# A two-layer DeltaNet and attention block on one core: shared decay buffers, decay exponents on ACT, the late modulation as one DVE product

## Chip, cores and metric

One core of one Trainium2 chip. The metric is the device time of one execution in microseconds (us), and the median of several runs is compared. The profile is of one execution. Its engines are PE (TensorE, matmul; PEld is its weight load), DVE (VectorE), ACT (ScalarE), POOL (GpSimd) and SP (SyncE, which here only issues DMAs). ACT issues DMAs too, from its own instruction queue.

## What is computed

Two layers over 256 context and 256 latent tokens, D = 2048. Layer 0 mixes with a bidirectional gated DeltaNet (16 key heads, 32 value heads, width 128), layer 1 with differential attention. What matters here is this:

```
mod   = silu(c) @ ada_w[i] + ada_b[i]          # (D) @ (D, 3D): shift, scale, gate; once for c, once for c_ctx
h     = rmsnorm(x) * (1 + scale) + shift       # per layer, latent and context tokens
g     = -exp(a_log) * softplus(...)            # log decay, per token and head
gc    = cumsum(g) within a chunk
decay = exp(gc[i] - gc[j]) where i >= j, else 0
lower = beta * (k k^T) * decay, strictly lower # inverted as (I + lower)^-1
a     = (q k^T) * decay
x     = x + gate * mixer(h)
```

## The kernel before, in words

All is kept transposed: features on the 128 partitions, the 512 tokens (context, then latent) on the free axis. Every large product is three fp32r matmuls: a weight tile is split into a high part (ACT, a cast at L185) and a low part (POOL, or for every other piece after the loop DVE, L187).

**Start** (L284 to L330). The 16 tiles of x are loaded on SP (L298), squared on ACT and summed on DVE to the norm. The shift and scale of layer 0 are computed on TensorE by `ada_pair` (L173) from 64 loads of 512 KB (`ada_load`, L164, on SP); sixteen pairs, two of them before every two tiles of h. Three projections run along while h is made (L313).

**Gates** (`gates`, L361). From a small projection come beta and the cumulated log decay: `gct` (the cumulated decay minus lnb, L449) and `lnb` (L443), both with tokens on partitions, and the decay rows in DRAM (`gc_d`, L435).

**The DeltaNet loop** (L486 to L997). Four streams are interleaved by `Drive`, a small event simulation written into the kernel: it emits the matmul groups in the order of their modelled readiness and rank. `stream_m` (L728) makes the masked matrices m for each head pair g and half and inverts 16x16 blocks on DVE (`block_inv`, L703); `stream_lev` (L760) widens the inverse on TensorE over PSUM tiles iv (R on DVE at L786, T and U on ACT at L803 and L804); `stream_at` (L807) makes q k^T times decay; `stream_b` (L832) runs the chunk recurrence over PSUM tiles sb and so (y and yb, x0, x, S: L879 to L926). `filler` (L652) runs the input projections in what is left of TensorE. Both `stream_m` and `stream_at` call `decay` (L682) for each of 4 chunks and 16 head pairs, 128 times in all. It loads the decay rows of four (direction, head) pairs by two broadcast DMAs on SP (L686), subtracts and clamps in four DVE instructions with per-partition operands (L692), and takes the exponential on ACT (L694). The tile has one buffer per caller (tags grm and gra); `scaled` (L697) is its last reader, on DVE.

**The late modulation.** The gate of layer 0 and all of layer 1's modulation, 64 column tiles of 128, are not needed early. `ada_pieces` (L150) cuts each column tile into eight pieces of 256 inputs. A piece is loaded on ACT's queue into one of two buffers (tag ra, L135), along with the two condition rows, broadcast, for every four column tiles (L158); for each of the two conditions POOL multiplies (L138) and ACT sums with an accumulating copy (L139). That is 64 x 8 = 512 loads and 1024 products. 24 column tiles are emitted among the loop's streams with the lowest rank but one (L995), 24 between the output projection's tiles (L1041, L1067), 16 between the heads of layer 1 (L1146).

**After the loop.** The output projection in two halves (L1032, L1053), the norm and h of layer 1 (L1078), layer 1 with eight heads (L1131 to L1207), its output projection and the final norm.

**What orders the work.** The program is written in the Tile layer. It allocates buffers by tag (as many at a time as `bufs` says), places the waits, and orders each engine's instructions ahead of time: a list scheduler with a timeline simulation (L1287) takes the ready instruction that stands first in the program. So work of low rank or of a later stage can be placed early on an engine that is idle in that simulation. On the chip every queue then runs strictly in that order.

Of the kernel before, what the change touches and what calls it, by code (L numbers as in the profile page):

```python
# [10 lines left out]
F32 = mybir.dt.float32  # L11
F32R = mybir.dt.float32r
F16 = mybir.dt.float16
BF16 = mybir.dt.bfloat16
AF = mybir.ActivationFunctionType
# [5 lines left out]
P = 128  # L21
T = 512
NCH = 4
# [38 lines left out]
def body(ctx, tc, D, d, out):  # L62
# [70 lines left out]
    def ada_part(l, ct, q, cr, acc, NK):  # L133
        r = wp.tile([P, NK], F32, tag="ra", name=f"aw{l}_{ct}_{q}", bufs=2)
        nc.scalar.dma_start(r, d["adaw"][l, ct, :, q * NK:(q + 1) * NK])  # L135
        for s in range(2):
            pr = wp.tile([P, NK], F32, tag="rp", name=f"rp{l}_{ct}_{q}{s}", bufs=1)
            nc.gpsimd.tensor_tensor(pr, r, cr[:, s], ALU.mult)  # L138
            nc.scalar.activation(pr, pr, AF.Copy, accum_out=acc[:, s, q:q + 1])  # L139

# [9 lines left out]
    def ada_pieces(lcs):  # L150
        NK = 256
        NQ = D // NK
        accs = {lc: cst.tile([P, 2, NQ], F32, name=f"al{lc[0]}_{lc[1]}", tag="al", bufs=5) for lc in lcs}
        for q in range(NQ):
            yield
            cr = wp.tile([P, 2, NK], F32, name=f"cr{lcs[0]}{q}", tag="cr", bufs=2)
            for s in range(2):
                nc.scalar.dma_start(cr[:, s], sc_d[s:s + 1, q * NK:(q + 1) * NK].to_broadcast([P, NK]))  # L158
            for lc in lcs:
                ada_part(*lc, q, cr, accs[lc], NK)  # L160
        for lc in lcs:
            ada_fin(*lc, accs[lc])
# [98 lines left out]
    gp = gp_cm.__enter__()  # L261
    gct, eg, kd, egl, lnb = (gp.tile([P, NCH, 2, HV], F32, name=n) for n in ("gct", "eg", "kd", "egl", "lnb"))
    zt = gp.tile([P, P], F16, name="zt")
# [32 lines left out]
    with tc.high_priority():  # L296
        for kt in range(KT):
            nc.sync.dma_start(xt[kt], d["xT"][:, kt])  # L298
        nc.scalar.activation(acc0, xt[0], AF.Square)
# [6 lines left out]
        for k0 in range(0, KT, SK):  # L306
            for kind in range(2):
                pr = kind * HKT + k0 // 2
                ada_pair(0, pr, ada_load(0, pr, ta, "ar", 8), (gq, tr)[np_ % 2](), ta)
                np_ += 1  # L310
# [50 lines left out]
    def gates(ps):  # L361
# [65 lines left out]
        for a in range(2):  # L427
            p3 = (gq, tr)[a]()
            for c in range(2):
# [12 lines left out]
        nc.vector.tensor_scalar(t2[0], bt, -1.0, None, ALU.mult)  # L442
        nc.vector.tensor_scalar(lnb, softplus(0), -1.0, None, ALU.mult)  # L443
        tc.keep_in_program_order(nc.scalar.activation(eg, p1v, AF.Exp))
# [3 lines left out]
        nc.vector.tensor_copy(raw, p1v)  # L448
        nc.vector.tensor_tensor(gct, raw, lnb, ALU.subtract)  # L449
        e = tl("be", sh)  # L450
# [231 lines left out]
    def decay(g, c, s, tag):  # L682
        gr = dl.tile([P, 4, P], F32, tag=tag, name=f"{tag}{g}{c}", bufs=1)
        gsrc = gc_d[c].rearrange("(d h) i -> d h i", d=2)
# [4 lines left out]
        for u in range(4):  # L689
            dd, h = divmod(u, 2)  # L690
            j = 2 * g + h
            nc.vector.tensor_scalar(gr[:, u], gr[:, u], gct[:, c, dd, j:j + 1], lnb[:, c, dd, j:j + 1],  # L692
                                    ALU.subtract, ALU.min)
        nc.scalar.activation(gr, gr, AF.Exp)  # L694
        return gr
# [7 lines left out]
    def block_inv(g, half, m16):  # L703
# [7 lines left out]
        pr = dl.tile([64, 16, 16], F32, tag="bP", name=f"bP{nm}", bufs=1)  # L711
        TU = dl.tile([64, 2, 16, 16], F16, tag="bT", name=f"bT{nm}", bufs=1)
        nc.vector.tensor_scalar(X[:32], bk[:32].rearrange("p j i -> p i j"), -1.0, None, ALU.mult)
# [587 lines left out]
```

## Time and profile before

| | us |
|---|---|
| median of 3 runs (3129.51 to 3135.29) | 3134.51 |
| the profiled execution | 3130.73 |
| its span, first to last instruction | 3128.9 |
| PE busy in the span | 2817.8 |
| POOL, DVE, ACT busy | 2012.8, 1955.8, 1872.4 |
| mean granted clock of TensorE | 0.963 |

The span is what the engines show; about 2 us of the execution lie around it. Busy times are unions over an engine's instructions, and DMA-issuing instructions are not counted as busy. A wait row says how long an engine sat idle before instructions of one group, and what ended that. The wait is put down to what came last. A granted clock of 1.00 is 2.4 GHz, 0.50 would be 1.2 GHz.

### The profile page before, as it was taken

What the parts mean: (1) busy time and instruction counts of PE and PEld (TensorE: products, weight loads), DVE (VectorE), ACT (ScalarE), POOL (GpSimd) and SP (SyncE); (2) the same over time, 40 slices, a digit from 0 to 9 for tenths busy, and PEclk for the clock granted to TensorE, in tenths of its full rate; (3) what the DMA queues carried; (4) which work ended last, traced back from release to release, by engine and by line L of the source; (5) the groups of instructions that cost most, each with busy time, mean ns of one, the idle gap of its engine ahead of it and who ended that gap; (6) DMA issues with size and microseconds to landing.
All of it is one profiled execution on the core that took longest, in us unless ns stands there. A gap on an engine that the chain in (4) does not pass through costs nothing. (4 is left out here: it accounts for less than half of the span.)

```text
span 3128.9 us, 52162 instructions
## 1 busy us (share of the span) xinstructions
PE 2817.8 (90%) x16178; PEld 2239.7 (72%) x16178; DVE 1955.8 (63%) x4287; ACT 1872.4 (60%) x5466; POOL 2012.8 (64%) x2370
## 2 busy tenths in 40 slices
PE   5788988988988988988898888899998999999998
PEld 2465767766766766766776666688687888888897
DVE  2178688688678677688578678632335654544454
ACT  4345766766766666766666666654556666654353
POOL 2366777777767777777777777466565666752334
PEclk8899999999999999999999999999999999999999
DMA  9646555456545545445456445667744555543345
GB/s 339 235 100 139 124 127 130 127 119 135 126 118 133 134 116 139 117 125 139 117 126 137 121 120 138 173 178 207 238 147 120 162 155 162 160 142 109 115 130 164
DMA packets 510312, 457.03 MB, mean 146 GB/s; under 512 B 241744, under 2 KB 380752, under 8 KB 510032
## 3 DMA queue, kind: packets, MB, share of 16 engines
q1 hardware_dynamic: 299456, 342.48, 37.7%
q10 hardware_dynamic: 210576, 111.22, 14.9%
q8 instruction: 127, 2.08, 0.3%
q14 instruction: 153, 1.25, 0.1%
HBM read 427.18 MB, written 26.36 MB: 145 GB/s over the span
## 5 line engine op out<-in xcount | busy, mean ns | idle before, releaser
L139 ACT ACTIVATE rp<-rp 128x256 f32<-128x256 f32 x1024 | 426.8, 417 | 298.2 <-POOL rp L138 292.6
L717 DVE TENSOR_TENSOR bP<-bX,bY 64x1 f32<-64x1 f32 (+14 forms) x480 | 225.1, 469 | 22.0 <-ACT bY L715 14.2
L139 ACT ACTIVATION_READ_ACCUMULATOR rp<-rp 128x1 f32 x1024 | 194.2, 190 | 0.0
L692 DVE TENSOR_SCALAR grm<-grm,gct,lnb 128x128 f32<-128x128 f32 x256 | 133.2, 563 | 84.8 <-DMA grm<-gc_d 84.1
L692 DVE TENSOR_SCALAR gra<-gra,gct,lnb 128x128 f32<-128x128 f32 x256 | 116.0, 493 | 85.0 <-DMA gra<-gc_d 84.7
L786 DVE TENSOR_TENSOR R<-iv,lv 128x512 f16<-128x512 f32 x192 | 127.1, 680 | 28.7 <-PE iv L83 28.5
L83 PEld LDWEIGHTS <-m 128*128 128x128 f16 x1024 | 76.2, 100 | 78.7 <-issue 71.5
L694 ACT ACTIVATE grm<-grm 128x512 f32<-128x512 f32 x64 | 40.3, 630 | 129.1 <-DVE grm L692 125.3
L719 DVE TENSOR_REDUCE bY<-bP 64x1 f32<-64x1 f32 (+14 forms) x480 | 108.6, 226 | 8.0
L750 POOL TENSOR_TENSOR ma<-ma,cs 128x512 f32<-128x512 f32 x64 | 86.5, 1352 | 32.3 <-DVE ma L700 30.0
L83 PE MATMUL iv<-T,m 128*128 128x128 f16 x768 | 74.3, 225 | 32.5 <-DMA T<-tu_d 19.1
L83 PE MATMUL iv<-U,R 128*128 128x128 f16 x768 | 76.9, 227 | 28.5 <-DVE R L786 26.4
L694 ACT ACTIVATE gra<-gra 128x512 f32<-128x512 f32 x64 | 40.4, 631 | 103.8 <-DVE gra L692 103.7
L83 PEld LDWEIGHTS <-R 128*128 128x128 f16 x768 | 48.8, 101 | 70.9 <-DVE R L786 37.9
L224 DVE TENSOR_TENSOR hlo<-mh,hhi 128x512 fp32r<-128x512 f32 x32 | 25.9, 833 | 114.9 <-ACT hhi L223 87.8
L83 PE MATMUL sb<-yb,uf 128*128 128x128 bf16 x512 | 55.5, 225 | 32.5 <-DVE yb L910 20.9
L803 ACT CAST T<-iv 128x512 f16<-128x512 f32 x128 | 74.1, 579 | 16.2 <-PE iv L83 12.5
L753 POOL TENSOR_TENSOR ml<-ma,m 128x512 bf16<-128x512 f32 x64 | 75.3, 1177 | 6.2 <-ACT m L752 5.3
L83 PEld LDWEIGHTS <-uf 128*128 128x128 f16 x512 | 36.2, 100 | 57.3 <-issue 52.1
L804 ACT CAST U<-iv 128x512 f16<-128x512 f32 x128 | 75.9, 593 | 0.0
L83 PE MATMUL so<-x,at 128*128 128x128 f32 x512 | 73.3, 280 | 0.3 <-DVE sz L966 0.3
L83 PEld LDWEIGHTS so<-x,at 128*128 128x128 f32 x512 | 67.2, 195 | 2.6 <-PE sb L83 0.4
(2767 smaller groups left out, 11393.0 us busy)
## 6 DMA issues: line engine op xcount, KB each, us to landing
aw<-in_adaw_dram ACTq DMA_DIRECT2D x512, 128.0 KB, 2.9
ar<-in_adaw_dram SPq DMA_DIRECT2D x64, 512.0 KB, 7.5
grm<-gc_d SPq DMA_DIRECT2D x128, 128.0 KB, 4.4
gra<-gc_d SPq DMA_DIRECT2D x128, 128.0 KB, 4.5
mb_d<-m ACTq DMA_DIRECT2D x32, 256.0 KB, 4.9
U<-tu_d SPq DMA_DIRECT2D x128, 64.0 KB, 2.9
T<-tu_d SPq DMA_DIRECT2D x128, 64.0 KB, 3.3
yd<-sz SPq DMA_DIRECT2D x32, 256.0 KB, 3.7
```

The costliest lines, as they stand in the source:

```text
L83: nc.tensor.matmul(o, l, r, start=start, stop=stop)
L139: nc.scalar.activation(pr, pr, AF.Copy, accum_out=acc[:, s, q:q + 1])
L224: nc.vector.tensor_tensor(hlo(kt), t, hhi[:, kt, :].bitcast(F32), ALU.subtract)
L692: nc.vector.tensor_scalar(gr[:, u], gr[:, u], gct[:, c, dd, j:j + 1], lnb[:, c, dd, j:j + 1], ALU.subtract, ALU.min)
L694: nc.scalar.activation(gr, gr, AF.Exp)
L717: nc.vector.tensor_tensor(pr[:, :i, :i], X[:, i, :i].unsqueeze(1).to_broadcast([64, i, i]), Y[:, :i, :i].rearrange("p j c -> p c j"), ALU. ...
L719: nc.vector.tensor_reduce(Y[:, i, :i], pr[:, :i, :i], AX.X, ALU.add)
L750: nc.gpsimd.tensor_tensor(ma, ma, ident.unsqueeze(1).to_broadcast([P, 4, P]), ALU.add)
L753: nc.gpsimd.tensor_tensor(ml[:, :, k], mv, m16[:, :, k], ALU.subtract)
L786: nc.vector.tensor_tensor(R, quad(pp), lvb(n), ALU.mult)
L803: nc.scalar.copy(Tm, quad(pt))
L804: nc.scalar.copy(U, quad(pu))
```

## The change

- `ada_part`: the weight loads and the condition rows are issued on SP; product and sum are one DVE instruction with an accumulated output. POOL and ACT have no part in it any more.
- `decay`: all callers share the tag gr with three buffers. ACT makes the exponent with four Relu instructions (scale -1, bias gct), then exp with scale -1. The clamp at lnb becomes a clamp at 0; it only concerns masked entries. The tile lnb goes, and softplus(0) is added where it was subtracted.
- Start: x is loaded alternately on SP and ACT; the first two modulation pairs stand ahead of the norm in the program.
- One of two PSUM tiles in the gates comes from the tag iv and not tr; the tile TU of `block_inv` shares the buffer of the product tile bP.

```diff
--- before.py
+++ after.py
@@ -132,11 +132,10 @@
 
     def ada_part(l, ct, q, cr, acc, NK):
         r = wp.tile([P, NK], F32, tag="ra", name=f"aw{l}_{ct}_{q}", bufs=2)
-        nc.scalar.dma_start(r, d["adaw"][l, ct, :, q * NK:(q + 1) * NK])
+        nc.sync.dma_start(r, d["adaw"][l, ct, :, q * NK:(q + 1) * NK])
         for s in range(2):
             pr = wp.tile([P, NK], F32, tag="rp", name=f"rp{l}_{ct}_{q}{s}", bufs=1)
-            nc.gpsimd.tensor_tensor(pr, r, cr[:, s], ALU.mult)
-            nc.scalar.activation(pr, pr, AF.Copy, accum_out=acc[:, s, q:q + 1])
+            nc.vector.scalar_tensor_tensor(pr, r, 1.0, cr[:, s], ALU.mult, ALU.mult, accum_out=acc[:, s, q:q + 1])
 
     def ada_fin(l, ct, acc):
         m = cst.tile([P, 2], F32, name=f"am{l}_{ct}", tag="am", bufs=2)
@@ -155,7 +154,7 @@
             yield
             cr = wp.tile([P, 2, NK], F32, name=f"cr{lcs[0]}{q}", tag="cr", bufs=2)
             for s in range(2):
-                nc.scalar.dma_start(cr[:, s], sc_d[s:s + 1, q * NK:(q + 1) * NK].to_broadcast([P, NK]))
+                nc.sync.dma_start(cr[:, s], sc_d[s:s + 1, q * NK:(q + 1) * NK].to_broadcast([P, NK]))
             for lc in lcs:
                 ada_part(*lc, q, cr, accs[lc], NK)
         for lc in lcs:
@@ -259,7 +258,7 @@
 
     gp_cm = pool("gp", side="right")
     gp = gp_cm.__enter__()
-    gct, eg, kd, egl, lnb = (gp.tile([P, NCH, 2, HV], F32, name=n) for n in ("gct", "eg", "kd", "egl", "lnb"))
+    gct, eg, kd, egl = (gp.tile([P, NCH, 2, HV], F32, name=n) for n in ("gct", "eg", "kd", "egl"))
     zt = gp.tile([P, P], F16, name="zt")
     nc.vector.memset(zt, 0.0)
     t0_cm = pool("t0", reuse_waits="tile")
@@ -295,7 +294,9 @@
     ta = ta_cm.__enter__()
     with tc.high_priority():
         for kt in range(KT):
-            nc.sync.dma_start(xt[kt], d["xT"][:, kt])
+            (nc.sync, nc.scalar)[kt % 2].dma_start(xt[kt], d["xT"][:, kt])
+        for pr in (0, HKT):
+            ada_pair(0, pr, ada_load(0, pr, ta, "ar", 8), (gq, tr)[pr > 0](), ta)
         nc.scalar.activation(acc0, xt[0], AF.Square)
         for kt in range(1, KT):
             sq = ta.tile([P, T], F32, tag="mh", name=f"sq{kt}", bufs=2)
@@ -304,7 +305,7 @@
         nc.scalar.copy(rrow0, rstd_rows(acc0, T, iv, ta.tile([P, 4, P], F32, name="rr_dg0")))
         np_ = 0
         for k0 in range(0, KT, SK):
-            for kind in range(2):
+            for kind in range(2 if k0 else 0):
                 pr = kind * HKT + k0 // 2
                 ada_pair(0, pr, ada_load(0, pr, ta, "ar", 8), (gq, tr)[np_ % 2](), ta)
                 np_ += 1
@@ -425,7 +426,7 @@
         nc.vector.tensor_tensor(g, w, wide(ea), ALU.mult)
         tri = lambda dd: cs[:, C_TRI + dd * P:C_TRI + (dd + 1) * P]
         for a in range(2):
-            p3 = (gq, tr)[a]()
+            p3 = (gq, iv)[a]()
             for c in range(2):
                 for dd in range(2):
                     q = 2 * c + dd
@@ -440,13 +441,13 @@
                 mm(p1v[:, c, dd, :], tri(dd), g[:, c, dd, :])
         mm(p1[:, n:2 * n], ones, fl(g))
         nc.vector.tensor_scalar(t2[0], bt, -1.0, None, ALU.mult)
-        nc.vector.tensor_scalar(lnb, softplus(0), -1.0, None, ALU.mult)
+        nlnb = softplus(0)
         tc.keep_in_program_order(nc.scalar.activation(eg, p1v, AF.Exp))
         tc.keep_in_program_order(nc.scalar.dma_start(sc_d.rearrange("s (p i) -> (s p) i", i=W2), rc))
         nc.scalar.activation(egl, p1[:, n:2 * n].rearrange("p (c d h) -> p c d h", c=NCH, d=2), AF.Exp)
         raw = tl("raw", sh)
         nc.vector.tensor_copy(raw, p1v)
-        nc.vector.tensor_tensor(gct, raw, lnb, ALU.subtract)
+        nc.vector.tensor_tensor(gct, raw, nlnb, ALU.add)
         e = tl("be", sh)
         nc.scalar.activation(e, bt, AF.Exp, scale=-1.0)
         nc.vector.tensor_scalar(e, e, 1.0, None, ALU.add)
@@ -680,7 +681,7 @@
         return t.rearrange("p (u i) -> p u i", u=4)
 
     def decay(g, c, s, tag):
-        gr = dl.tile([P, 4, P], F32, tag=tag, name=f"{tag}{g}{c}", bufs=1)
+        gr = dl.tile([P, 4, P], F32, tag="gr", name=f"{tag}{g}{c}", bufs=3)
         gsrc = gc_d[c].rearrange("(d h) i -> d h i", d=2)
         for dd in range(2):
             nc.sync.dma_start(gr[:, 2 * dd:2 * dd + 2, :],
@@ -689,9 +690,8 @@
         for u in range(4):
             dd, h = divmod(u, 2)
             j = 2 * g + h
-            nc.vector.tensor_scalar(gr[:, u], gr[:, u], gct[:, c, dd, j:j + 1], lnb[:, c, dd, j:j + 1],
-                                    ALU.subtract, ALU.min)
-        nc.scalar.activation(gr, gr, AF.Exp)
+            nc.scalar.activation(gr[:, u], gr[:, u], AF.Relu, scale=-1.0, bias=gct[:, c, dd, j:j + 1])
+        nc.scalar.activation(gr, gr, AF.Exp, scale=-1.0)
         return gr
 
     def scaled(o, gr, pg, s, nm):
@@ -709,7 +709,7 @@
         X = dl.tile([64, 16, 16], F32, tag="bX", name=f"bX{nm}", bufs=1)
         Y = dl.tile([64, 16, 16], F32, tag="bY", name=f"bY{nm}", bufs=1)
         pr = dl.tile([64, 16, 16], F32, tag="bP", name=f"bP{nm}", bufs=1)
-        TU = dl.tile([64, 2, 16, 16], F16, tag="bT", name=f"bT{nm}", bufs=1)
+        TU = dl.tile([64, 2, 16, 16], F16, tag="bP", name=f"bT{nm}", bufs=1)
         nc.vector.tensor_scalar(X[:32], bk[:32].rearrange("p j i -> p i j"), -1.0, None, ALU.mult)
         nc.vector.tensor_scalar(X[32:], bk[32:], -1.0, None, ALU.mult)
         nc.scalar.copy(Y, e16[:64])
```

## Rows read from the trace of the kernel before

**Rows 1.** The page's first part: busy us, share of the span, instructions

```profile
PE 2817.8 (90%) x16178; PEld 2239.7 (72%) x16178; DVE 1955.8 (63%) x4287; ACT 1872.4 (60%) x5466; POOL 2012.8 (64%) x2370
```

**Rows 2.** Stretches: length, then busy us of PE, PEld, DVE, ACT, POOL, clock, DMA, GB/s

```profile
0.00:170.00 170.00, 117.43 (x782) 70.15 (x783) 42.53 (x79) 67.93 (x163) 50.30 (x71) 0.85 0.76 267
...
300.00:2010.00 1710.00, 1525.15 (x9024) 1186.00 (x9023) 1281.26 (x2991) 1131.95 (x3475) 1244.89 (x1552) 0.96 0.52 128
2010.00:2390.00 380.00, 371.77 (x1632) 293.64 (x1631) 133.67 (x256) 202.60 (x615) 242.18 (x268) 0.99 0.63 189
...
2500.00:3020.00 520.00, 507.93 (x3005) 442.54 (x3005) 270.86 (x532) 278.69 (x726) 270.58 (x271) 1.00 0.45 140
```

**Rows 3.** TensorE's waits, 300 to 2010 us: us in total, times, longest

```profile
PE iv L83 <- DVE R L786: 26.5, 24, 3.3
...
PE iv L83 <- ACT T L803: 11.9, 12, 3.2
...
PE sb L83 <- DVE x L916: 4.6, 8, 1.4
...
PE pj L83 <- ACT g10khi L185: 2.7, 1, 2.7
```

**Rows 4.** The waits of all engines, 300 to 2010 us

```profile
ACT rp L139 <- POOL rp L138: 111.5, 161, 2.7
ACT grm L694 <- DVE grm L692: 106.9, 47, 4.7
ACT gra L694 <- DVE gra L692: 97.0, 47, 4.2
DVE gra L692 <- DMA gra<-gc_d: 79.4, 51, 4.2
DVE grm L692 <- DMA grm<-gc_d: 73.9, 42, 5.9
```

**Rows 5.** Stretches again: tile rp alone (ACT, POOL), then line 692 alone (DVE)

```profile
300.00:2010.00 1710.00, 306.36 (x1204) 475.08 (x602) 0.96 0.52 128
2010.00:2390.00 380.00, 101.17 (x399) 160.44 (x199) 0.99 0.63 189
...
300.00:2010.00 1710.00, 220.44 (x456) 0.96 0.52 128
```

**Rows 6.** Line 135's instructions (duration ns min/median/max) and who waited for them

```profile
L135 ACTq DMA_DIRECT2D aw<-in_adaw_dram x512: 333/339/1987, 0.7 to 2775.2; - x171
...
  POOL rp L138: 35.9, 27
```

**Rows 7.** The same view of lines 418, 1181, 143, 951 and 578

```profile
L418 DVE SCALAR_TENSOR_TENSOR gt_at<-gt_at,gt_at x7: 409/426/953, 161.5 to 167.2; 128x256 f32<-128x256 f32 x7
...
L1181 DVE SCALAR_TENSOR_TENSOR pe<-pe,rc,pe x16: 740/752/1652, 2501.7 to 3024.2; 128x512 f32<-128x512 f32 x16
...
L143 DVE TENSOR_REDUCE am<-al x64: 147/160/172, 372.2 to 2783.3; 128x2 f32<-128x16 f32 x64
...
L951 ACT ACTIVATE jko<-O,rq x128: 384/398/425, 347.1 to 2099.9; 128x128 f32<-128x128 f32 x128
...
L578 ACT ACTIVATE jk<-tr x64: 254/277/313, 185.4 to 1866.6; 128x128 f32<-128x128 f32 x64
```

**Rows 8.** SyncE's queue: its waits over the whole span

```profile
SPq L686 <- DVE at L700: 93.8, 40, 6.2
...
SPq L119 <- POOL g0v0lo L187: 41.1, 3, 34.0
```

**Rows 9.** DMA issues: engine, count, KB each, median us to landing

```profile
grm<-gc_d SPq DMA_DIRECT2D x128, 128.0 KB, 4.4
...
tu_d<-bT ACTq DMA_DIRECT2D x64, 32.0 KB, 3.2
```

**Rows 10.** Stretches of the start, columns as in rows 2

```profile
0.00:20.00 20.00, 0.00 (x0) 0.00 (x0) 10.83 (x23) 11.61 (x19) 0.20 (x4) 1.00 0.83 273
30.00:130.00 100.00, 79.90 (x616) 45.28 (x608) 7.76 (x12) 42.08 (x110) 40.85 (x55) 0.81 0.99 352
```

## The prediction

> **What bounds the kernel now.** I read the busy shares first, then the stretches of the span, then TensorE's waits in the longest stretch, then the waits of every engine there. TensorE is busy 2817.8 us of 3128.9, so at most some 310 us can be won anywhere [rows 1]. The stretches say where its idle time lies: 53 us in the start (117 busy of 170), 185 us in the DeltaNet loop (1525 of 1710), 8 and 12 us in the output projection and in layer 1 [rows 2]. So this is a loop question. In the loop no other engine is near its end: DVE is busy 75%, POOL 73%, ACT 66%. TensorE's gaps there are many and short: the five longest rows that end on DVE (R, yb, gm, S, x) run from 26.5 to 4.6 us and sum to 72.2 us, the seven that end on ACT (T, yb, x and four weight casts) run from 11.9 to 2.7 us and sum to 42.1 us [rows 3].
>
> Why are ACT and DVE late at 66 and 75%? Because they stand still in the middle of their in-order queues. ACT stood 111.5 us for POOL's product and 106.9 + 97.0 us for DVE's exponents; DVE stood 79.4 + 73.9 us for the DMA of the decay rows [rows 4]. With that, ACT is taken 1132 + 315 = 1447 us of 1710 (85%) and DVE 1281 + 153 = 1434 us (84%). All else sits behind: on ACT the weight casts and the T, U, yb and x casts, on DVE R, yb, S and x, which TensorE waits for.
>
> **The change, part by part**, against the profiled execution: 3130.73 us, of which 3128.9 are the span. The median shown, 3134.51, is 3.8 us above it; I add that at the end.
>
> *Modulation, removed.* In the loop ACT loses 306 us and POOL 475 us, for 602 products [rows 5]. ACT's 512 weight loads, 0.339 us of its queue each [rows 6], go to SP; two products share a load, so about 301 of them, 102 us that was not counted as busy, fall into the loop. The 256 loads of the condition rows move along.
>
> *Modulation, added.* Per product one 128x256 instruction on DVE with both inputs in SBUF and an accumulated sum. The nearest row is the softplus recurrence, the same instruction and shape without the sum: 0.426 us in the median [rows 7]. A sum on DVE is not in this trace; if it is read out by an instruction of its own, a tiny DVE instruction is the measure: 0.160 [rows 7]. I take 0.43 + 0.16. From below it is 0.43 alone; from above the columns pass twice: L1181, the same instruction with 512 columns, takes 0.752, so 256 more cost 0.33, and 0.43 + 0.33 + 0.16 = 0.92. To the middle comes contention: L1181 is 1.652 at most, against a median of 0.752 [rows 7], while POOL is busy 52% [rows 2]. POOL falls from 73% to about 45% in the loop; I add 0.10 and get 0.69 us (0.43 to 0.92).
>
> A rule of the Trainium skill bears on that tail: SBUF — State Buffer, in its list of what contends, says that a DVE instruction with two SBUF inputs and a GpSimd instruction that reads SBUF exclude each other, and the later one waits until the other is done. It speaks against this change, which makes of a POOL product a DVE product that meets POOL's weight splits. The maxima of L1181 agree with it, its median does not: most don't wait. At the rule's worst each product waits for a whole POOL instruction, 475/602 = 0.79 us by [rows 5]: 602 x 0.79 more puts DVE at some 1890 us, 180 more than the loop has, where the sum below has a gain.
>
> *Decay exponents.* DVE loses 220 us [rows 5] and the 153 us of standing for DMA. ACT gains four Relu of 128x128 per decay with a per-partition bias. The nearest row with a per-partition operand and an SBUF source takes 0.398, one from PSUM without it 0.277 [rows 7]. With the 456 instructions seen in the loop that is 126 to 181 us; I take 181, since source and operand are alike. Three shared buffers let SP issue a decay's row loads up to two decays ahead, and it no longer stands 93.8 us for DVE's last reader of the single buffer [rows 8]. The wait is now ACT's, with the casts behind it: 0 to 153 us. I take 30, for a lead of two decays (128 of them in 1710 us, so 27 us) is well over the landing of 4.4 us [rows 9].
>
> *Small edits.* One DVE instruction less in the gates; a PSUM tile from another tag; TU in bP's buffer, so that the next block inversion waits until TU's stores have landed, 3.2 us [rows 9]. There are 32 inversions, 53 us apart, and that hides it; without this cover it would be 3 us each, on a part of DVE's queue that TensorE does not wait for at once. I cost these at nothing.
>
> *Start.* The first 20 us move 273 GB/s; from 30 to 130 us it is 352, with the DMA engines full [rows 10]. x on two queues, with the first two modulation pairs ahead in program order, fills that hole: 79 GB/s x 20 us = 1.58 MB, or 4.5 us at 352 GB/s. Bounds 0 and 4.5; I take 4, since that stretch is full to its end. Next in line is the work on h.
>
> *The sum.* ACT in the loop: 1132 - 306 + 181 + 30 = 1037 us, 61% instead of 85%. If the delay in a queue goes with its taken over its free share (an estimate, from 85/15 to 61/39), TensorE's 42 us become 12: -30. DVE, if the modulations keep their pace: 1281 - 220 + 602 x 0.69 = 1476 us, 86% after 84%: 72 us become about 84, +12. POOL is no longer above half, and the splits it makes come earlier: -4. The clock, granted at 0.96 in the loop and at 0.99 to 1.00 in the stretches where TensorE hardly idles [rows 2]: with 22 of 185 us of idle time gone, I give back an eighth of that difference of 1525 us, -7. The loop: -29. After it, the products leave POOL's and ACT's queues; DVE, busy 35% in the output projection [rows 2], takes 199 products [rows 5] x 0.69 = 137 us of 380 and stays at 71%. Of the 20 us idle there I take back 6. So -4 - 29 - 6 = -39 us: 3130.7 - 39 = 3092, and 3.8 for the median: 3096. I round to **3095 us**, by itself 3060 to 3122.
>
> **The rivals.**
>
> *DVE becomes the bound (slower).* Place: DVE's queue in the loop. A planner fills idle engines from far ahead, and only two weight buffers hold the products back; ACT, which shared their pace, no longer does. If all 995 that are left at 300 us crowd into the loop, DVE is at 1281 - 220 + 995 x 0.59 = 1648 us, 96%. It decides from about 92% on: each R and yb then queues behind a product and its load. If the 72 us grow two and a half times, that is +108 against -51 of the other terms: about 3190 us. For it: DVE has TensorE's longest rows [rows 3] and gets the work. Against it: 373 us of work and standing leave DVE, and the products stand last in the program order of their stage. Chance 0.14.
>
> *The product at half rate (slower).* At 0.92 us, 602 products put DVE at 1615 us, 94%, in the same place: 72 us become some 150, which ends at about 3165 us. The Trainium skill has it so: Vector Engine (DVE) Microarchitecture Reference, Points that are easy to get wrong, says that this instruction loses half its throughput when both sources lie in SBUF and are not bf16. The trace does not agree for the form without the sum (0.426 for 256 columns); the form with it is not there. Chance 0.06.
>
> *SP blocks.* The weight loads leave a queue that made POOL wait 35.9 us in all [rows 6], for one that stood up to 34.0 us at a time behind a wait for POOL [rows 8]. A late load now holds R and yb on DVE. If those waits triple, DVE is at 1476 + 108 us, 93%, unless its products thin out: most of the gain goes, about 3125 us. Chance 0.08.
>
> *Hidden anyway.* TensorE's gaps follow the chain between TensorE and DVE and not ACT's standing; only start and tail give: about 3124 to 3134 us. For it: the DVE rows are the larger [rows 3]. Chance 0.14.
>
> *More than costed.* DVE's standing was what made R and yb late. If half of the 72 us goes instead of 12 coming, and the clock comes up by half the difference, that is another -48 - 23: about 3024 us. Chance 0.14.
>
> **How the numbers follow.** The forecast keeps 0.44. The range, 3018 to 3170, reaches from the large gain through the half-rate case and leaves out most of the DVE bound and the tail of the large gain. 0.2%, 6.3 us, is about what a measurement of this kernel can tell from no change. Faster (under 3128): 0.44 + 0.14 + about half of the hidden and of the SP case, 0.11 = 0.69. Slower: 0.20 and 0.02 of the SP case = 0.22. Within: the other 0.09.
>
> **What would show it.** Right: ACT's standing for POOL's product and DVE's exponents gone, ACT taken near 60% and POOL near 45% in the loop; a product and its sum near 0.69 us; weight casts and T and yb casts of ACT down to about 12 us in TensorE's waits; the loop some 30 us shorter. Wrong: products of 0.9 us; DVE over 92% in the loop with R, yb, gm, S and x above 100 us; DVE standing for the weight loads by the hundred us; ACT standing more than 100 us for the decay rows; the first projections no earlier.

## The result and the profile after

The changed kernel takes 3269.7 us in the median of 4 runs (3265.7 to 3276.5), the kernel before 3134.5: a ratio of 1.0437 [1.0416, 1.0458]. It is slower by 4.4%, where the forecast had 1.3% faster, and it lies outside the range. The profiled execution has a span of 3267.2 us, 138.3 more.

The page's first part, after, answers to [rows 1]:

```profile
PE 2876.4 (88%) x16178; PEld 2263.7 (69%) x16178; DVE 2112.8 (65%) x5822; ACT 1593.0 (49%) x3930; POOL 1274.9 (39%) x1346
```

ACT and POOL shed 279 and 738 us, DVE gained only 157, and TensorE is busy for 88% of the span instead of 90%. Its busy time still grew by 58.6 us, for the same 16178 matmuls, while its mean granted clock fell from 0.963 to 0.945. So of the 138.3 us, 80 are more idle time of TensorE, and 59 are matmuls that took longer. The stretches, with the columns of [rows 2], show where the time went:

```profile
300.00:2010.00 1710.00, 1449.95 (x8132) 1104.31 (x8132) 1368.23 (x4231) 912.48 (x2451) 777.07 (x874) 0.93 0.57 138
300.00:1860.00 1560.00, 1310.74 (x7274) 997.17 (x7274) 1264.58 (x3984) 813.04 (x2186) 701.65 (x786) 0.92 0.58 142
1860.00:2281.00 421.00, 393.44 (x2305) 306.57 (x2304) 259.42 (x613) 239.57 (x609) 165.27 (x187) 0.97 0.47 115
```

From 300 to 2010 us TensorE gets 8132 matmuls done, 892 fewer than before, at a clock of 0.93 against 0.96. The loop's last yb (L910) starts at 2274.5 us and not at 2084.0: the loop is 190 us longer, and what lies behind it 52 us shorter. Why 1860 stands there as a border, the same view of the tile rp alone shows (DVE, clock, DMA share, GB/s):

```profile
300.00:2010.00 1710.00, 498.09 (x1912) 0.93 0.57 138
1860.00:2281.00 421.00, 1.32 (x8) 0.97 0.47 115
2281.00:3267.00 986.00, 0.00 (x0) 0.99 0.38 123
```

All products are done by 1864 us; before, they ran to 2783. 956 of them (half of 1912, each has a read-out of the sum) fall into the loop's stretch, where [rows 5] had 602. While they last, DVE is busy 81% and TensorE 84%; once they are gone, 62% and 93%.

The waits of all engines from 300 to 2010 us, as in [rows 4], and then those of TensorE, as in [rows 3]:

```profile
DVE rp L138 <- DMA aw<-in_adaw_dram: 232.3, 172, 6.2
...
ACT gra L693 <- DMA gra<-gc_d: 107.1, 64, 5.2
ACT jko L951 <- DVE O L937: 84.7, 23, 7.5
ACT grm L693 <- DMA grm<-gc_d: 76.7, 57, 4.0
...
ACT yb L884 <- DVE y L879: 38.6, 17, 5.9
PE iv L83 <- DVE R L786: 50.5, 36, 4.3
PE sb L83 <- ACT yb L884: 22.2, 14, 4.1
PE sb L83 <- DVE S L926: 17.5, 8, 4.8
PE iv L83 <- ACT T L803: 11.0, 10, 3.3
PE sb L83 <- DVE x L916: 10.6, 7, 3.2
PE sb L83 <- DVE yb L910: 9.0, 9, 3.2
PE so L83 <- DVE x L916: 7.6, 5, 2.6
PE gq L83 <- DVE gm L699: 6.9, 9, 1.4
```

ACT's standing for POOL's product and for DVE's exponents is gone, as foretold. In its place stands one row that no part of the sum had: DVE waits 232 us for the modulation's weights. TensorE's waits for R went from 26.5 to 50.5 us. ACT, with more room than before, stands in its turn for DVE's O and y, 84.7 and 38.6 us. SyncE's queue, the view of [rows 8], shows the other end of the same loads:

```profile
SPq L135 <- DVE rp L138: 316.2, 247, 4.3
SPq L135 <- DMA aw<-in_adaw_dram: 139.5, 109, 4.3
...
SPq L135 <- DVE bY L719: 81.6, 62, 3.6
SPq L135 <- DVE bP L717: 58.6, 46, 4.2
```

L135 issues the weight loads, and these rows say how long SP's queue waits before it: some 600 us in all, until one of the two buffers is free. Before, SP had no such row, and ACT's queue, which issued these loads, none either.

### The profile page after: what moved, and what is told of

The parts are those of the page before. It is cut to its first block, busy times and chain, and to the rows that moved or that the text cites. A ratio compares the mean times of both kernels' runs of the same rounds, so it can differ in the third digit from the quotient of the medians.

```text
span 3267.2 us, 51329 instructions
## 1 busy us (share of the span) xinstructions
PE 2876.4 (88%) x16178; PEld 2263.7 (69%) x16178; DVE 2112.8 (65%) x5822; ACT 1593.0 (49%) x3930; POOL 1274.9 (39%) x1346
## 5 line engine op out<-in xcount | busy, mean ns | idle before, releaser
L717 DVE TENSOR_TENSOR bP<-bX,bY 64x1 f32<-64x1 f32 (+14 forms) x480 | 215.6, 449 | 19.3 <-DMA tu_d<-bT 9.9
L693 ACT ACTIVATE gra<-gra,gct 128x128 f32<-128x128 f32 x256 | 88.6, 394 | 132.2 <-DMA gra<-gc_d 128.2
L693 ACT ACTIVATE grm<-grm,gct 128x128 f32<-128x128 f32 x256 | 88.4, 395 | 94.8 <-DMA grm<-gc_d 89.2
L83 PEld LDWEIGHTS <-R 128*128 128x128 f16 x768 | 49.8, 102 | 99.8 <-DVE R L786 61.1
L951 ACT ACTIVATE jko<-O,rq 128x128 f32<-128x128 f32 x128 | 51.0, 398 | 93.3 <-DVE O L937 92.6
L753 POOL TENSOR_TENSOR ml<-ma,m 128x512 bf16<-128x512 f32 x64 | 83.4, 1303 | 26.9 <-ACT m L752 22.1
L870 POOL TENSOR_TENSOR kx<-ktok,kd 128x256 f32<-128x256 f32 x96 | 69.0, 739 | 31.3 <-PE sb L83 26.9
L83 PE MATMUL sb<-S,kT 128*128 128x256 f32 x192 | 54.3, 406 | 21.0 <-DVE S L926 17.5
L83 PE MATMUL sb<-x,kx 128*128 128x128 f32 x384 | 56.3, 291 | 10.9 <-DVE x L916 10.6
```

The source lines that it names most:

```text
L83: nc.tensor.matmul(o, l, r, start=start, stop=stop)
L693: nc.scalar.activation(gr[:, u], gr[:, u], AF.Relu, scale=-1.0, bias=gct[:, c, dd, j:j + 1])
L717: nc.vector.tensor_tensor(pr[:, :i, :i], X[:, i, :i].unsqueeze(1).to_broadcast([64, i, i]), Y[:, :i, :i].rearrange("p j c -> p c j"), ALU. ...
L753: nc.gpsimd.tensor_tensor(ml[:, :, k], mv, m16[:, :, k], ALU.subtract)
L870: nc.gpsimd.tensor_tensor(kx[:, dd], ktok[:, cd[dd]].unsqueeze(1).to_broadcast([P, 2, P]), kd[:, cd[dd], dd, 2 * g:2 * g + 2].unsqueeze(2) ...
L951: nc.scalar.activation(jk, O[:, c, h], AF.Square, scale=rq[:, c0 + c:c0 + c + 1], accum_out=ss[:, c, h:h + 1])
```

## The experiments

"Before" is run beside each experiment on the same chip; its median there is 3120 to 3122 us. So I compare by ratios to it. An interval is given where a version was executed four times or more; a ratio without one is of a single execution. On this scale the changed kernel stands at 1.0437. The versions in which a product reads two columns or the condition rows alone, or in which loads or products are missing, don't compute the reference's modulation: they only serve to measure.

### Which part of the change costs the time

**The changed kernel with the old product** (POOL multiplies, ACT sums, loads on ACT's queue):

```diff
-        nc.sync.dma_start(r, ...)                      # and the condition rows
+        nc.scalar.dma_start(r, ...)
-            nc.vector.scalar_tensor_tensor(pr, r, 1.0, cr[:, s], ..., accum_out=acc[:, s, q:q + 1])
+            nc.gpsimd.tensor_tensor(pr, r, cr[:, s], ALU.mult)
+            nc.scalar.activation(pr, pr, AF.Copy, accum_out=acc[:, s, q:q + 1])
```

> The changed kernel with the late modulation put back as it was: product on POOL, sum on ACT, loads on ACT's queue; the decay change, the start and the small edits stay. If the modulation on DVE costs the time (whether by its work, by its standing for loads, or by the loads on SP), this is faster than the kernel before: 3050 to 3120 us, a head pair of the loop near 105 us. If the decay exponents on ACT cost it (ACT stood 217 us for the decay rows in the changed kernel), it stays above 3180 us, a head pair near 125 us.

**Before with the new product alone**, the reverse edit:

> The kernel before with the modulation change alone: product and sum on DVE, loads on SP; decay as before. If the modulation costs the time: 3220 to 3330 us, with DVE standing over 200 us for the loads of the weights, on top of its standing for the decay rows. If the decay part costs it: 3120 to 3150 us.

Measured: 3067.0 us, 0.9812 [0.9795, 0.9828], and 3259.6 us, 1.0440. With the new product the kernel takes the same time with and without the rest of the change, 4.4% more than before; with the old product the rest gains 1.9%. So, in shares of the time before, the new product costs 4.4% by itself and 6.2% beside the rest of the change, whose gain it swallows. The new product alone made DVE stand 107.7 us for the weights, half of the 200 that were expected. In the version with the old product TensorE's waits in its loop (300 to 2007 us) are:

```profile
PE iv L83 <- DVE R L787: 10.8, 15, 2.9
PE sb L83 <- DVE S L924: 8.4, 3, 5.2
PE sb L83 <- ACT yb L885: 8.0, 6, 4.1
```

R has come down from 26.5 us [rows 3]. What of the rest earns this, three further versions of it part: **the exponent back on DVE** (with the three shared buffers kept), **two decay buffers instead of three**, and **the old start**.

```diff
-            nc.scalar.activation(gr[:, u], gr[:, u], AF.Relu, scale=-1.0, bias=gct[...])
-        nc.scalar.activation(gr, gr, AF.Exp, scale=-1.0)
+            nc.vector.tensor_scalar(gr[:, u], gr[:, u], gct[...], 0.0, ALU.subtract, ALU.min)
+        nc.scalar.activation(gr, gr, AF.Exp)
```

> The run with the old product (3067 us), with the decay exponents back on DVE but the three shared buffers kept. If the third buffer is what gained: DVE stands under 60 us for the decay rows (168 us in the kernel before) and the time is 3050 to 3085 us. If moving the exponents to ACT is what gained: 3100 to 3130 us.

```diff
-        gr = dl.tile([P, 4, P], F32, tag="gr", ..., bufs=3)
+        gr = dl.tile([P, 4, P], F32, tag="gr", ..., bufs=2)
```

> The run with the old product, with two shared buffers for the decay rows in place of three. If the third buffer lets loads start earlier and shortens ACT's standing for the rows (151 us with three): ACT stands 200 us or more and the time is 3085 to 3120 us. If the standing does not come from the number of buffers: within 0.5% of the run with three, a ratio to the kernel before of 0.977 to 0.987.

```diff
-            (nc.sync, nc.scalar)[kt % 2].dma_start(xt[kt], d["xT"][:, kt])
+            nc.sync.dma_start(xt[kt], d["xT"][:, kt])
-        for pr in (0, HKT):
-            ada_pair(0, pr, ...)
-            for kind in range(2 if k0 else 0):
+            for kind in range(2):
```

> The run with the old product, with the start put back (x on SP alone, the modulation pairs behind the norm). If the new start is worth the 4 us that the sum gave it: 0.1 to 0.2% slower than the run with the old product, that is a ratio to the kernel before of 0.982 to 0.984. If it is worth nothing or costs something, 0.979 to 0.981.

Measured: 3157.0 us (1.0112); 3078.1 us, 0.9863 [0.9846, 0.9879]; 3064.2 us, 0.9816 [0.9785, 0.9847]. With the exponents on DVE, the waits of all engines show that shared buffers don't keep DVE from standing:

```profile
DVE gra L694 <- DMA gra<-gc_d: 83.4, 61, 5.4
DVE grm L694 <- DMA grm<-gc_d: 75.4, 58, 4.7
```

In the kernel before, the same view of the whole span has

```profile
DVE gra L692 <- DMA gra<-gc_d: 84.7, 56, 4.2
DVE grm L692 <- DMA grm<-gc_d: 84.1, 50, 5.9
```

So the gain is the exponent's move off DVE, some 3% from 1.0112 to 0.9812. With the exponent on DVE the version is 1.1% slower than before, and above both ranges expected for it: something in the shared buffers, the start or the small edits costs time then, and which was not tried. The third buffer is worth half a per cent. For the start no difference shows; 4 us, which the prediction gave it, are 0.13% and lie inside the interval.

### Which way the new product costs it

All that follows changes only the late modulation of the changed kernel.

**The loads on ACT's queue**, the product staying on DVE (`nc.scalar.dma_start` for `nc.sync.dma_start` in both places):

> The changed kernel with the loads of the late modulation back on ACT's queue; the product stays on DVE. If SP's queue, which stood some 600 us ahead of these loads, is the cause: 3080 to 3160 us. If DVE is the cause, through the work it took on or through its standing for loads with two buffers: 3230 to 3300 us, DVE still standing over 150 us for the loads.

**A narrow product**, two of 256 columns:

```diff
-            nc.vector.scalar_tensor_tensor(pr, r, 1.0, cr[:, s], ...)
+            nc.vector.scalar_tensor_tensor(pr[:, :2], r[:, :2], 1.0, cr[:, s, :2], ...)
```

> The changed kernel with the product cut to 2 of its 256 columns (the late modulation is then not the reference's): the loads, their two buffers and the wait of DVE stay, most of DVE's work goes. If the standing for loads is what costs, whatever the work: 3180 to 3260 us, DVE still standing over 200 us for loads. If the work of the products is what costs: 3040 to 3110 us.

Measured: 3259.5 us (1.0440), with DVE standing 259.7 us for aw; and 3275.4 us (1.0494), above both ranges. Neither SP's queue as such nor DVE's work is the price. With the loads on ACT's queue, ACT stands for DVE's products instead of SP, with its casts behind the loads:

```profile
ACT T L803 <- DVE rp L138: 23.2, 11, 3.4
```

The page and the waits of the narrow product:

```profile
PE 2868.4 (88%) x16178; PEld 2274.5 (69%) x16178; DVE 1837.0 (56%) x5822; ACT 1592.0 (49%) x3930; POOL 1205.9 (37%) x1346
```

```profile
DVE rp L138 <- DMA aw<-in_adaw_dram: 386.9, 257, 6.7
```

DVE loses 276 us of work and stands 137 us more than in the changed kernel (249.5 us over its whole span); the time doesn't fall.

**Four weight buffers.** To make room, the decay rows have two, and two small constants lie elsewhere:

```diff
-        r = wp.tile([P, NK], F32, tag="ra", ..., bufs=2)
+        r = wp.tile([P, NK], F32, tag="ra", ..., bufs=4)
```

> The changed kernel with four buffers for the loaded weights in place of two; to make room the decay rows get two buffers in place of three and two constants move to a pool that closes earlier. If DVE's standing for loads is the cause: that row falls from 250 us to under 100 us and the time to 3130 to 3190 us. If the sheer crowding of products in DVE's queue is the cause: the standing falls but the products come still earlier in the loop, and the time stays at 3230 to 3300 us.

**The products in the order of the program**, each behind the DVE instruction emitted last:

```diff
+            with tc.issue_after(mark[0].ins):     # R, x, xx or y, whichever came last
                 nc.vector.scalar_tensor_tensor(pr, r, 1.0, cr[:, s], ...)
```

> The changed kernel, with each product on DVE kept behind the last DVE instruction that the program emitted before it (R in the loop, the residual after it, y in layer 1), in issue order only; two buffers for the loads as changed. If products that run ahead and crowd the loop are the larger cause, beside the standing for loads: 3060 to 3150 us, fewer than 500 of the 1024 products in the loop, head pairs near 110 us, and the output projection and layer 1 no longer than in the kernel before. If two buffers and DVE's standing are the cause wherever the products lie: 3180 to 3260 us, DVE standing over 200 us for the loads, part of it after the loop.

**Both together:**

> Both at once: products kept in program order, four buffers for the loads (two for the decay rows). If standing for loads and crowding together are all that the product on DVE costs: 3040 to 3090 us, as fast as the old product or faster, DVE standing under 40 us for loads. If the work on DVE itself is dear: 3110 us or more.

Measured: 3143.9 us (1.0070), 3264.4 us (1.0456) and 3137.5 us, 1.0048 [1.0030, 1.0066]. Four buffers give back 3.7% of the 4.4%, inside the range for DVE's standing as the cause; the order by itself gives nothing (just above both ranges). Both together stay where "the work on DVE itself is dear" was expected, but narrow products, above and below, contradict that reading. The start of the last yb shows that order only moves the cost (before 2084.0, after 2274.5, four buffers 2125.0); this is its row in the version in program order:

```profile
L913 DVE TENSOR_TENSOR yb<-y,sb x48: 667/677/689, 314.6 to 2059.2; 128x512 bf16<-128x512 f32 x48
```

Its loop is 25 us shorter than that of the kernel before, but its products run to 3094 us, and what lies behind the loop takes 1203 us instead of 1045. DVE's waits in the versions with two buffers in program order, and with four buffers in the planner's order:

```profile
DVE rp L141 <- DMA aw<-in_adaw_dram: 280.7, 191, 4.8
```

```profile
DVE rp L138 <- DMA aw<-in_adaw_dram: 40.3, 29, 3.4
```

Up to here the theory was that an engine which TensorE needs stands for the loads. Two runs put that standing on POOL: DVE multiplies condition rows alone, and POOL looks at two columns of each load.

```diff
+        nc.gpsimd.tensor_tensor(lk, r[:, :2], cr[:, 0, :2], ALU.mult)
-            nc.vector.scalar_tensor_tensor(pr, r, 1.0, cr[:, s], ...)
+            nc.vector.scalar_tensor_tensor(pr, cr[:, 1 - s], 1.0, cr[:, s], ...)   # and with [:2] throughout
```

> The changed kernel with full products that read the condition rows in place of the loaded weights (not the reference's modulation); a POOL instruction of 2 columns reads each load, so that the loads keep their pace and POOL waits for them. DVE keeps its work and no longer stands for the weights. If the standing is what costs: 3050 to 3140 us. If the work and the crowding cost: 3190 us or more.

> Both cuts at once: 2 columns, and no load that DVE waits for (not the reference's modulation). This is the floor of the changed kernel when the late modulation costs DVE next to nothing: 3000 to 3070 us, and the cuts of the two runs before should add up to about its distance from 3270 us. If the decay part or the loads themselves cost time, it stays above 3100 us.

Measured: 3283.1 us (1.0519) and 3305.5 us (1.0590), both far above what the theory gave. In the first, POOL stands 272.9 us for aw and DVE only 45 us, for condition rows: with DVE nearly free of standing, nothing is gained. In the second, POOL stands 446.8 us for aw, and DVE 326 us for condition rows, which come down SP's queue behind the weights. Both runs still have the loads, and a reader of them.

### Loads without a reader

**No loads**, 1024 narrow products on the condition rows (the edit above without `lk` and without `r`); **loads that nobody reads** (the same, with the load into its two buffers); and **small loads** that nobody reads:

```diff
-        nc.sync.dma_start(r, d["adaw"][l, ct, :, q * NK:(q + 1) * NK])
+        nc.sync.dma_start(r[:, :16], d["adaw"][l, ct, :, q * NK:q * NK + 16])
```

> The changed kernel without the late modulation's 512 weight loads, and its 1024 products on 2 of 256 columns of the condition rows alone: the output lacks the late modulation. It is the floor for every theory. Standing theory (an engine that TensorE needs stands in its order for loads that two buffers hold back): nothing stands, so this ends at or under the version with the old product (3067 us): 3000 to 3070. If anything else of the change costs the time, it stays above 3150.

> As the run before, but all 512 weight loads are issued into their two buffers, and no engine reads them: the output lacks the late modulation. Standing theory: no engine waits for them, so the time is that of the run without loads within some 25 us. Rival, the loads themselves cost it (their traffic beside the other transfers, or SP's queue, which still issues them one behind the other): near the 3305 us of the run in which POOL looked at each load.

> As the run in which nobody reads the weights (3265 us), but each of its 512 loads fetches 16 of 256 columns, a sixteenth of the bytes: same number of issues, same two buffers, same waits of SP's queue for the load before; the output lacks the late modulation. It parts the two ways in which unread loads could cost the 141 us against the run without loads (3124 us). Theory, SP's queue stands for the load before, with the decay rows and other loads behind it: the landing is mostly latency and falls by a third at most, so 3220 to 3260. Rival, the traffic: 3120 to 3150.

**No late modulation at all**, the sums set to zero:

> The changed kernel without any of the late modulation: no loads, no condition rows, no products; the sums are set to zero once per column tile. The floor. Theory, products and loads cost time by being early in queues that the loop needs, not by their sum: this ends near 3000 to 3050, under the version with the old product (3067 us), and the version with 1024 narrow products and no loads (3124 us) stood some 80 us above it for those small instructions alone. Rival, the loop's pace is set by something else of the change (the exponents on ACT behind DVE): the floor is itself at 3067 or above.

Measured, each against before: no modulation 2984.6 us, 0.9554 [0.9522, 0.9586]; no loads 3124.2 us, 1.0013 [0.9997, 1.0029]; small loads 3232.8 us, 1.0350 [1.0324, 1.0376]; full loads that nobody reads 3264.9 us, 1.0464 [1.0433, 1.0494]. No loads lies between the two expected ranges, no modulation below both. No engine reads the weights in the last two, and with full loads all of the 4.4% is there. That alone does not clear DVE. The narrow products still read the condition rows, and those are issued on SP behind the weight loads. DVE's waits for them (one row for each tile cr) add up to 105 us without loads, but to 219 us with full and 221 us with small ones; the longest after the start, with full loads:

```profile
DVE rp L138 <- DMA cr(1, 40)2_32400<-sc_d: 9.0, 1, 9.0
```

So here a reader still stands, for another load. SP's queue, first with full loads, then with small ones:

```profile
SPq L135 <- DMA aw<-in_adaw_dram: 359.6, 256, 6.1
```

```profile
SPq L135 <- DMA aw<-in_adaw_dram: 305.6, 221, 6.1
```

A load into a buffer must wait until the load before the last has landed there, and in SP's strict order the condition rows, the decay rows, the projections' weights and the block inverses' round trip through DRAM wait with it. A sixteenth of the bytes takes away a sixth of that standing, and leaves 3.4% of the 4.5% that the loads cost: only some 1% is the traffic. That the rest is the wait, and not the 512 issues, was not tried by itself; four buffers, which keep the issues and gave back 3.7%, speak for the wait. Nor is it shown which of the transfers behind the loads makes TensorE late. The stretch in which these loads run, then a later one without them (columns of [rows 2]): no loads,

```profile
300.00:1100.00 800.00, 682.08 (x3916) 524.03 (x3915) 621.84 (x2921) 440.44 (x1189) 340.26 (x414) 0.94 0.53 120
1100.00:1900.00 800.00, 741.11 (x4419) 585.47 (x4420) 504.62 (x1188) 498.87 (x1338) 397.06 (x480) 0.96 0.39 97
```

full loads without a reader,

```profile
300.00:1100.00 800.00, 611.76 (x3326) 465.74 (x3324) 532.16 (x2724) 375.58 (x1003) 290.33 (x353) 0.89 0.67 171
1100.00:1900.00 800.00, 739.57 (x4387) 574.93 (x4386) 523.89 (x1343) 500.43 (x1351) 391.20 (x473) 0.97 0.42 105
```

small loads without a reader,

```profile
300.00:1100.00 800.00, 624.19 (x3383) 473.00 (x3382) 543.08 (x2850) 379.55 (x1023) 296.09 (x362) 0.89 0.53 115
```

and no modulation at all:

```profile
300.00:1100.00 800.00, 748.64 (x4507) 586.63 (x4505) 514.51 (x1211) 505.72 (x1372) 402.50 (x484) 0.97 0.39 98
```

Wherever loads and products are gone, TensorE does about 4400 to 4500 matmuls in 800 us; beside them 3300 to 3400, with ACT and POOL less busy too and the clock down to 0.89. Narrow products without loads lie between, at 3916.

**Four buffers and the narrow product**, and **the full product on condition rows beside loads that nobody reads**:

> Four weight buffers, and the product on 2 of 256 columns: the output lacks most of the late modulation. It tells what the 70 us are that are left between four buffers with the full product (3144 us) and the old product (3067 us). If they are DVE's work, some 0.4 us less for each of 1024 products: 3070 to 3100. If they are what is left of the standing, which narrow products don't shorten (with two buffers they didn't): 3130 to 3170.

> All 512 loads issued and read by no engine, the full 256-column product on the condition rows: DVE has the whole work and no standing for weights; the output lacks the late modulation. Standing theory: 20 to 70 us above the run with narrow products that nobody stands for, for the work alone, and so under 3144 us. Rival, the work is the cost: above 3200.

Measured: 3166.2 us, 1.0148 [1.0127, 1.0170], and 3321.0 us, 1.0643 [1.0619, 1.0667]. With four buffers, less work brings no gain (DVE then stands 171.6 us for aw instead of 40.3). Beside unread loads, the full width adds 1.8%, and the time lies where "the work is the cost" was expected; but 1.8% is the smaller part.

The last run parts what the narrow ones could not. DVE stands only 83 us for condition rows in it, a third of the changed kernel's 258 us (aw and condition rows), and yet it is the slowest of all. The version with four buffers has the same full product and 46 us of such standing, at 1.0070. What differs is SP's queue, here first without a reader, then with four buffers:

```profile
SPq L135 <- DMA aw<-in_adaw_dram: 451.4, 274, 5.8
```

```profile
SPq L135 <- DVE rp L138: 201.8, 189, 3.7
```

So DVE's standing is not needed for the loss. But SP's standing is no measure of it either: with four buffers all its waits at L135 still come to some 360 us, nearly all for DVE, as many as with unread full loads at 1.0464, where they are for a load to land.

### What the runs add up to

From 0.9554 without late modulation, the old product adds 2.6% and the new one 8.8%. Of the 8.8%, by the runs that add one thing each, 4.6% come with 1024 narrow products and their condition rows, 3.4% with 512 small loads that SP's queue stands for, 1.1% with their bytes, 1.8% with the full width; with readers, the loads run until 1859 us and not 1150, and 2.1% less than this sum is left. What is shown is that the loss comes with loads into two buffers in a queue that the loop shares, and is neither DVE's work nor, by itself, its standing. The rest is my reading: the planner sees room on DVE and sends products and loads as fast as two buffers let it, and on the chip an in-order queue that the loop needs stands for each, SP's or ACT's for the buffer, DVE's or POOL's for the load. No trace shows the planner's simulation; that all products are done by 1864 us fits. The old chain over POOL and ACT spread its products to 2783 us, and in the version with the old product no queue stands for L135.

Not settled: each edit also makes the planner order the other work anew, so the shares are no exact parts, and an order that happens to be worse is a rival that no run excludes; it is unlikely, since five versions with two buffers and a DVE product that reads the weights lie close together, at 1.0437 to 1.0494. Whether the 4.6% are the small instructions or the condition rows' two buffers (SP stands 164.6 us for rp behind them, at L155) was not tried apart; nor was it tried why four buffers still end 2.6% above the old product, beyond that less work on DVE did not help. Loads issued by a third engine were not tried.

The fastest version that computes the reference is the changed kernel with the old product: 3067.0 us, 0.9812 of before (0.9816 with the old start, no difference).

## Why the prediction was wrong

The step that failed is the DVE term, "if the modulations keep their pace … 72 us become about 84, +12". Their pace was not kept: 956 products and not 602 fell into the stretch, and while they ran DVE was busy 1264.58 us and stood 232 more for their loads, of 1560: 96% and not 86%. TensorE's rows for R, yb, gm, S and x, counted in full, went from 73.5 us to 105.5 (R 50.5, S 20.9, x 18.2, yb 9.0, gm 6.9), and not to 84. Those of the kernel before that [rows 3] leaves out are, beside a second row of S with 1.3 us,

```profile
PE sb L83 <- DVE yb L910: 20.9, 17, 3.3
PE gq L83 <- DVE gm L699: 10.7, 8, 3.3
PE sb L83 <- DVE S L923: 9.5, 4, 3.8
```

Under this lies a term that the sum put at nothing: who waits for the weight loads once their consumer and their issue sit in queues that the loop needs. Only the rival "SP blocks" priced it, at three times 35.9 us on DVE. The runs showed 232 us of it on DVE and some 600 us on SP, and four buffers took 3.7% of the time away. The ACT term, −30, failed as well: all rows that end on ACT went from 61.1 to 121.1 us, of which the weight casts from 28.8 to 78.8 (with four buffers 71.1, so they don't mark the loss).

- **The product's price** was too high, 0.69 us: 498.09 us / 956 = 0.52, read-out included. By the prediction's own form, 956 x 0.52 = 498 us instead of 602 x 0.69 = 415, the term is too small by 83 us; the number of products and the waits did it, not the price.
- **ACT.** Its standing for POOL and for DVE's exponents went as said; for the decay rows it stands 183.8 us, and not 30 (bounds 0 to 153). Taken share: (912 + 184)/1710 = 64%, near the 61%. But the lower load made nothing earlier: T kept 11.0 of its 11.9 us in TensorE's waits, yb and the weight casts rose. For yb a cause is in the rows, DVE's y. The step from taken share to delay fails even without any late modulation: ACT is taken 70% of that loop, (1029 + 139)/1660, and TensorE's rows on ACT sum to 61.7 us, where the kernel before has 61.1.
- **POOL** came to 45%, as said; TensorE's rows on it went from 18.8 to 17.8 us, a gain of 1 and not 4. **The clock** went the other way, 0.96 to 0.93 in the stretch.
- **The start**: 332 GB/s in the first 20 us and not 273, so three quarters of the hole were filled. What it is worth can't be told from zero (0.9816 against 0.9812).
- **After the loop**: −52 us, and not −6. No product was left there; without any late modulation that part is 30 us shorter than before, so the products explain some 30 of the 52, and the rest is open.
- **The decay half** by itself gained 1.9%: this is the mechanism of the rival "more than costed", that DVE's standing was what made R and yb late, at a good half of its size (−1.9%, where 3024 us would be −3.5%). In the version with the old product TensorE's R row fell to 10.8 us; with the exponent back on DVE it is 24.0.
- **"DVE becomes the bound"** is the rival that came, with place, crowding (956 of 995) and sign as written; at +57 us it was priced at less than half of the 138. That its 96% came out is luck: it counted work alone, where DVE worked 81% and stood 15%. Nor is the cause DVE's work, as the narrow product shows. **"SP blocks"** named the other half, at +30 us of lost gain: unread loads alone cost 4.5%, and still 3.4% with a sixteenth of the bytes.
- **"The product at half rate"** is refuted, in the view of line 138 (ns min/median/max):

```profile
L138 DVE SCALAR_TENSOR_TENSOR rp<-aw,cr(0, 32)0_2419 x8: 408/424/985, 184.3 to 192.2; 128x256 f32<-128x256 f32 x8
L138 DVE DVE_READ_ACCUMULATOR rp<-aw,cr(0, 32)0_2419 x8: 75/81/82, 184.6 to 192.5; 128x1 f32 x8
```

0.424 us with the sum, against 0.426 without it [rows 7]. The Trainium skill's rule (Vector Engine (DVE) Microarchitecture Reference, Points that are easy to get wrong) would make it twice that; the trace does not agree.

## What to carry to other kernels

Before moving filler work to an engine with room, ask what its loads do in the queues: with two buffers and a planner that fills every gap, each load can become a wait of an in-order queue that the critical loop shares, whether or not anyone reads it. A slow consumer on side engines may be the brake that keeps such work spread (here it was, as I read it). How many buffers the loads had decided more than how much work the engine did: four instead of two gave 3.7%, products of two columns nothing. And look for an engine that stands for the input of work that another engine could do: the decay exponents' move off DVE gave 3%, though ACT then stood for the same rows.

## What was unexpected of the hardware

- The sum of a DVE product is read out in 0.08 us (row above), half of the 0.160 of the tiny DVE instruction taken as its measure, and it seems to cost no time of its own: in the timeline the read-out starts while the product is still on record, and the next instruction starts with it.

```profile
184.27 0.42 DVE L138 SCALAR_TENSOR_TENSOR rp<-aw,cr(0, 32)0_2419 128x256 f32<-128x256 f32 x1 [8.33 <-DMA cr(0, 32)0_2419<-sc_d]
184.62 0.08 DVE L138 DVE_READ_ACCUMULATOR rp<-aw,cr(0, 32)0_2419 128x1 f32 x1
184.62 0.42 DVE L420 SCALAR_TENSOR_TENSOR gt_O<-gt_O,gt_O 128x256 f32<-128x256 f32 x1
```

- A product of 2 columns is not nearly 128 times cheaper than one of 256. Without loads, the tile rp takes on DVE

```profile
300.00:920.00 620.00, 216.27 (x1718) 0.93 0.56 125
```

  so 0.25 us for product and read-out (859 of them), half of the 0.52 of the full width.
- A load of 8 KB and one of 128 KB (16 and 256 columns) hold the queue behind them almost equally: 305.6 and 359.6 us for 512 of them. From issue to landing it is 2.8 and 3.2 us in the median.
